# Stream 1 five weight chunks behind stream 0 at a layer's end and beginning, with seven weight buffers

## The chip, the cores and the metric

The kernel runs on one core of a Trainium2 chip. The metric is device time in microseconds (us) of one execution, less is better. Names of engines: TensorE is PE (its weight loads are PEld), VectorE is DVE, ScalarE is ACT, GpSimd is POOL, SyncE is SP.

## What is computed

Two requests of 128 tokens each run through the same two layers of width 2048: a context prompt (stream 0 here) and noisy latents (stream 1). A layer of the reference, cut to its matrix products:

```python
h = rms_norm(x, norm_w[l]) * (1 + scale) + shift          # scale, shift, gate: c @ w_mod[l]
parts = split_columns(h @ w_in[l])                        # 15872 columns
o_hg = hgrn_branch(...); o_at = attention(...); o_s5 = s5_branch(...)
merged = sum(sigmoid(merge) * (o @ w_br[l]))              # over the three branches
x = x + gate * (merged @ w_out[l])
```

After the last layer `rms_norm(x, final_norm)` is returned, with caches and states. `rms_norm` needs the sum of squares over all 2048 columns of a token, so neither the next layer nor the final scaling can start before the last output column of that token is there.

## The kernel before, in words

**Streams.** Tokens are rows: 128 partitions for stream `s = 0`, 128 for `s = 1`. Both use the same weights, so each weight chunk that is loaded serves both.

**A product in two parts.** Activations and weights in float32 are each split into a rounded part (`hi`, `wh`) and a remainder (`lo`, `wl`), and a product is the sum of three: `lo*wh`, `hi*wh`, `hi*wl` (lines 178 to 180). Weights move through the array (128x512), the activations are the stationary 128x128 operand.

**`gemm` (L160).** One group is 512 columns of the result for both streams, accumulated in two PSUM tiles `ps[0]`, `ps[1]` over `nk` chunks of 128 rows, 16 chunks for `w_in` and `w_out`. SP loads two chunks at a time (`raw`, 512 KB, three buffers, L168). ACT casts a chunk to `wh` (L138), DVE subtracts to get `wl` (L139), and PE does three products for stream 0 and then three for stream 1. `wh` and `wl` have four buffers each (`self.wp`, L68), so a chunk can be cast when the chunk four before it has been used by both streams.

**The end of a layer (L993 to L1025).** Four groups `n` of `w_out`. After each, and for each stream: DVE multiplies by the gate (`gb`, L1015) and adds the residual (L1016), ACT squares with a sum (`square`, L303). After `n = 3`, `token_rstd` (L305) reduces the eight partial sums of both streams in one 128x2 tile and computes 1/sqrt with one Newton step (`rstd`, L183: one ACT and six DVE instructions). In the last layer DVE also multiplies by `final_norm` (L1022) and `final` (L1060) scales the rows, stream 0 on DVE and stores on SP, stream 1 on ACT and stores on ACT's own queue.

**The beginning of a layer.** `normed` (L311) makes one quarter `q` of the normalised rows: DVE scales (`xn`, L322), PE transposes four blocks (L134), DVE (stream 0, L328) or ACT (stream 1, L330) applies scale and shift (`hf`), then cast and subtraction give `hh` and `hl`. Layer 1's first group is `("u", 0)`, 16 chunks, four for each quarter. In layer 0 the first groups are begun quarter by quarter (`begin`), since `w_mod` is still being loaded, so `group` finds `("u", 0)` already begun there.

**What sets the order.** The engines' queues are written by a planner that simulates the program: each instruction has a rank (`prio`, a smaller number goes first) and is placed when its operands are there in the plan. Weight loads and splits have `P_TOP` (1 million), the last column's chain and `token_rstd` `P_LAST` (0.9 million), `normed` `P_CHAIN` (2 million), S5 preparation 3 million, setup work `P_PREP` 5 million, weight products `P_PE` (6 million); within a rank program order decides. On the chip each engine runs its queue in order.

Of the kernel before, what the change touches and what calls it, by code (L numbers as in the profile page):

```python
# [15 lines left out]
ALU = mybir.AluOpType  # L16
AX = mybir.AxisListType
# [3 lines left out]
D = 2048  # L21
# [4 lines left out]
ROPE_THETA = 10000.0  # L26
NP = T // 2
RAW = 3
MB = 2
PTAGS = [(t, 2) for t in ("Bl", "S16", "ys")] + [(("k4", "k4"), 1)] + [("H8", 2)] * 4  # L30
STAGS = (("H8", 2),)
# [23 lines left out]
P_PE = 6_000_000  # L55
# [6 lines left out]
class Builder:  # L62
    def __init__(self, tc, ctx, io):
        self.tc, self.nc, self.io = tc, tc.nc, io
        self.seq = 0
        pool = lambda name, bufs, **kw: ctx.enter_context(tc.tile_pool(name=name, bufs=bufs, **kw))
        self.cp = pool("const", 1)
        self.wp = pool("weights", 4)  # L68
        self.sb = pool("sb", 1)
        self.bufs = dict(H8=4, Z8=2, Bl=1, CC=1, S16=1, uT=1, U2=1, ys=1, q4=2, kv=2,  # L70
                         mo=1, st=10, k2=6, k4=3, gt=4, sm=18, s5i=4, p=4, sb=1, sc=1, s5t=1)
        self.pg = pool("pg", 4, space=PSUM)
        self.pm = pool("pm", 2, space=PSUM)
        self.pb = pool("pb", 2, space=PSUM)
        self.dr = pool("scratch", 1, space=DRAM)
        self.uid = 0
# [80 lines left out]
        self.finish_side()  # L157
        self.side, self.side_rate, self.side_credit = gen, rate, 0.0

    def gemm(self, pieces, hi, lo, nk):  # L160

        nc = self.nc
        ps = [self.pg.tile([128, 512], F32, tag="g", name=self.nm("g")) for _ in range(2)]
        for kk, src in enumerate(pieces):
            self.side_work()
            with self.prio(P_TOP):
                raw = self.wp.tile([128, 2, 512], F32, tag="raw", name=self.nm("raw"), bufs=RAW)
                nc.sync.dma_start(raw, src.rearrange("p (a b) -> p a b", a=2))  # L168
            for j in range(2):
                with self.prio(P_TOP):  # L170
                    wh = self.wp.tile([128, 512], F32R, tag="wh", name=self.nm("wh"))
                    wl = self.wp.tile([128, 512], F32R, tag="wl", name=self.nm("wl"))
                    self.split_from(raw[:, j], wh, wl)
                k = 2 * kk + j
                with self.prio(P_PE):
                    for s in range(2):
                        sl = slice(s * 128, s * 128 + 128)
                        nc.tensor.matmul(ps[s], lo(k)[:, sl], wh, start=(k == 0), stop=False)  # L178
                        nc.tensor.matmul(ps[s], hi(k)[:, sl], wh, start=False, stop=False)  # L179
                        nc.tensor.matmul(ps[s], hi(k)[:, sl], wl, start=False, stop=(k == nk - 1))  # L180
        return ps

    def rstd(self, ssq, n, width):  # L183

        nc = self.nc
        v = self.ts("v", (128, n))
        y = self.ts("y", (128, n))
        r = self.ts("r", (128, n))
        w = self.ts("w", (128, n))
        nc.vector.tensor_scalar(v, ssq, 1.0 / width, EPS, ALU.mult, ALU.add)  # L190
        nc.scalar.activation(y, v, AF.Sqrt)
        nc.vector.reciprocal(r, y)
        nc.vector.tensor_mul(w, r, r)
        nc.vector.tensor_mul(w, w, v)
        nc.vector.tensor_scalar(w, w, -0.5, 1.5, ALU.mult, ALU.add)
        nc.vector.tensor_mul(r, r, w)
        return r
# [105 lines left out]
        self.nc.scalar.activation(junk, x[s][:, n * 512:(n + 1) * 512], AF.Square, accum_out=ssq[:, s, n:n + 1])  # L303

    def token_rstd(self, ssq):  # L305
        tot = self.ts("tot", (128, 2))
        self.nc.vector.tensor_reduce(tot, ssq, AX.X, ALU.add)
        r = self.rstd(tot, 2, D)
        return [r[:, s:s + 1] for s in range(2)]

    def normed(self, x, rs, q):  # L311

# [18 lines left out]
            sl = (slice(None), slice(q % 2 * 4, q % 2 * 4 + 4), slice(s * 128, s * 128 + 128))  # L331
            self.split_from(hf, self.hh[q // 2][sl], self.hl[q // 2][sl])

    def in_group(self, l, name, idx, k0=0, k1=16):

        pieces = [self.io["w_in"][l, GIDX[name, idx], kk] for kk in range(k0 // 2, k1 // 2)]
        return self.gemm(pieces, lambda k: self.hh[(k0 + k) // 8][:, (k0 + k) % 8],
                         lambda k: self.hl[(k0 + k) // 8][:, (k0 + k) % 8], k1 - k0)

    def add(self, dst, ps):  # L340
        with self.prio(P_TOP):
# [23 lines left out]
    def group(self, l, name, idx, func=None):  # L365
        dst = self.begun.pop((name, idx), None)
        if dst is None:
            ps = self.in_group(l, name, idx)
            dst = self.places(name, idx)
            for s in range(2):  # L370
                self.evac(ps[s], dst[s], func)
            return dst
        ps = self.in_group(l, name, idx, 8, 16)
        for s in range(2):
            self.add(dst[s], ps[s])
            if func is not None:
                with self.prio(P_TOP):
                    self.nc.scalar.activation(dst[s], dst[s], func)
        return dst
# [480 lines left out]
    def layer(self, l, x, rs):  # L860
        nc, io = self.nc, self.io
# [63 lines left out]
        for name, og in zip(("hg", "ag"), ogs):  # L925
            for hh in range(2):
                ps = self.in_group(l, name, hh)
# [7 lines left out]
        for b in range(3):  # L935
            if b == 1:
# [4 lines left out]
                def mods():  # L941
                    for p in parts:
                        yield from self.mod_part(*p, P_PE, tags, [("m", MB, MB)] * (8 // MB))

                if l + 1 < L:
                    self.start_side(mods(), MRATE[l] / MB)
                else:
                    self.start_side(self.gates, MRATE[l] / MB)
            if b == 2:
                sgs = {}  # L950
                for hh in range(2):
                    ps = self.in_group(l, "sg", hh)
# [4 lines left out]
            if b < 2:  # L957
                oh = self.t8("oh", (128, 8, 256), F32R)
                ol = self.t8("ol", (128, 8, 256), F32R)
                with self.prio(P_CHAIN):  # L960
                    for s in range(2):
                        for c in range(2):
                            tr = self.transpose4(ogs[b][s][c])
                            sl = (slice(None), slice(4 * c, 4 * c + 4), slice(s * 128, s * 128 + 128))
                            self.split_from(tr, oh[sl], ol[sl])
            else:
                early = [self.gate(l, b, n, ("st", "kv")[n]) for n in range(2)]
                oh, ol = self.s5_finish(l, ys, sgs)
                mt = [None] * 4
                m0 = self.t("S16", "mt", (128, 2, 8, 256), F32R)  # L970
                mt = [m0[:, 0], m0[:, 1]] + [self.t("H8", "mt", (128, 8, 256), F32R) for _ in range(2)]
            if merged is None:
                merged = [[self.t("st", "merged", (128, 512)) for _ in range(4)] for _ in range(2)]
            for n in range(4):
                gts = early[n] if b == 2 and n < 2 else self.gate(l, b, n, "gt")
                ps = self.gemm([io["w_br"][l, b, n, kk] for kk in range(4)],
                               lambda k: oh[:, k], lambda k: ol[:, k], 8)
                for s in range(2):
# [7 lines left out]
                    if b == 2:  # L986
                        with self.prio(P_CHAIN):
                            tr = self.transpose4(mb)
                            c = (4 * n) % 8
                            sl = (slice(None), slice(c, c + 4), slice(s * 128, s * 128 + 128))  # L990
# [3 lines left out]
        ssq = self.ts("ssq", (128, 2, 4))  # L994
# [4 lines left out]
                nc.gpsimd.dma_start(fn, bass.AP(src.tensor, src.offset, [[0, 128], [1, D]]))  # L999
        for n in range(4):  # L1000
            ps = self.gemm([io["w_out"][l, n, kk] for kk in range(8)],
                           lambda k: mt[2 * (k // 8)][:, k % 8], lambda k: mt[2 * (k // 8) + 1][:, k % 8], 16)
            sl = slice(n * 512, n * 512 + 512)
            if n == 3:
                self.finish_side()
                with self.prio(P_CHAIN):
                    nc.scalar.activation(self.ts("warm", (128, 1)), self.eye32[:, 0:1], AF.Sqrt)
            for s in range(2):
                with self.prio(P_LAST if n == 3 else P_TOP):
                    gb = self.t2("gb")  # L1010
                    nc.gpsimd.dma_start(gb, bass.AP(self.gate_d.tensor, self.gate_d.offset + (l * 2 + s) * D + n * 512,
                                                    [[0, 128], [1, 512]]))
                    xr = self.t2("xr")
                    nc.gpsimd.dma_start(xr, (io["x"] if l == 0 else self.x_d)[s][:, sl])
                    nc.vector.tensor_mul(gb, gb, ps[s])  # L1015
                    nc.vector.tensor_add(xn[s][:, sl], gb, xr)  # L1016
                    if l + 1 < L:
                        nc.gpsimd.dma_start(self.x_d[s][:, sl], xn[s][:, sl])
                    self.square(ssq, xn, s, n)
                if l + 1 == L:  # L1020
                    with self.prio(P_TOP + 500_000):
                        nc.vector.tensor_mul(xn[s][:, sl], xn[s][:, sl], fn[:, sl])  # L1022
        with self.prio(P_LAST):
            rs = self.token_rstd(ssq)
# [47 lines left out]
    def build(self):  # L1072
# [22 lines left out]
        for l in range(L):  # L1095
            x, rs = self.layer(l, x, rs)
            if l + 1 < L:
                def gates():
                    tags = itertools.cycle(MTAGS)
                    for p in (4, 5):  # L1100
                        yield from self.mod_part(L - 1, p, P_PE, tags, [("m", MB, MB)] * (8 // MB))

# [106 lines left out]
```

## Time and profile before

| | |
|---|---|
| median of 3 runs | 2330.3 us (2329.36 to 2330.72) |
| the profiled execution | 2331.88 us, its span 2330.1 us |
| granted TensorE clock, mean | 0.994 of full speed |
| PE busy | 2257.9 us, 97% |
| DVE busy | 1798.2 us, 77% |
| ACT busy | 1180.8 us, 51% |
| loaded from HBM | 474.36 MB, 207 GB/s over the span |

Times in the rows are us from the span's start. A busy share is an average; what an engine waited for, and in which stretch, is in the rows of the waits and of the timeline. `L178` is line 178 of the kernel; `wl<-raw,wh` is output from inputs; `x2` says how many instructions a row merges. In a timeline row the bracket at the end is the engine's idle time before it and what released it.

### The profile page before, as it was taken

The numbers are of one execution on the slowest core, as the hardware profiler recorded it, in microseconds if no ns is written. First come the engines' busy times: TensorE is split into PE (matmuls) and PEld (weight loads), VectorE is DVE, ScalarE is ACT, GpSimd is POOL, SyncE is SP. The second block draws the span as 40 slices with busy tenths as digits, with TensorE's granted clock in tenths as the row PEclk, the third lists the DMA queues.
The fourth block names the chain that finished last, engine by engine and source line by source line (L and its number), as shares of the span: only waits on it lengthen the run. The fifth ranks groups of instructions, "written<-read, shape, count | busy, mean of one in ns | idle before, by whom it ended". The sixth has DMA issues, their size and how long they took to land.

```text
span 2330.1 us, 38207 instructions
## 1 busy us (share of the span) xinstructions
PE 2257.9 (97%) x13192; PEld 1812.2 (78%) x13192; DVE 1798.2 (77%) x4835; ACT 1180.8 (51%) x2061; POOL 133.9 (6%) x244
## 2 busy tenths in 40 slices
PE   4999999999999999999998999999999999999997
PEld 2777877888887776887777888888878877887886
DVE  5856899799879868865565798899959968956555
ACT  3536645555554343544446565555564544454454
POOL 2000000100000100000010001000010010000000
PEclk9999999999999999999999999999999999999999
DMA  8994554355557878677874554454545677656765
GB/s 313 342 341 142 165 172 137 110 162 184 178 165 258 295 267 298 220 251 265 305 231 138 163 174 153 132 160 155 188 155 190 194 245 240 198 179 219 240 202 181
DMA packets 131490, 483.85 MB, mean 208 GB/s; under 512 B 17200, under 2 KB 17808, under 8 KB 126944
## 3 DMA queue, kind: packets, MB, share of 16 engines
q1 hardware_dynamic: 120528, 454.09, 58.2%
q0 software_dynamic: 9472, 23.97, 3.3%
q10 hardware_dynamic: 1296, 3.36, 0.4%
q8 instruction: 103, 1.69, 0.3%
q14 instruction: 91, 0.75, 0.1%
HBM read 474.36 MB, written 6.98 MB: 207 GB/s over the span
## 4 chain that ended last, share of the span: by engine, by line
PE 82%; DVE 8%; DMA 7%; issue 2%; ACT 1%; SPq 0%; POOL 0%; DVEq 0%; ACTq 0%; POOLq 0%
PE g L178 23%; PE g L180 23%; PE g L179 22%; DMA raw<-w_in 3%; DVE wl L139 3%; PE mod L274 3%; PE bu L816 3%; PE lv L432 2%; DMA raw<-w_br 2%; DMA wm<-w_mod 2%; PE tr L134 2%; PE yp L847 1%; DVE p L830 1%; DVE Sb L834 1%; ACT wh L138 1%
## 5 line engine op out<-in xcount | busy, mean ns | idle before, releaser
L138 ACT CAST wh<-raw 128x512 fp32r<-128x512 f32 x1344 | 819.4, 622 | 925.0 <-PE g L179 459.8
L139 DVE TENSOR_TENSOR wl<-raw,wh 128x512 fp32r<-128x512 f32 x1344 | 915.5, 689 | 368.5 <-ACT wh L138 319.1
L178 PE MATMUL g<-wh,hl 128*128 128x512 f32 x1984 | 785.1, 396 | 6.4 <-ACT wh L138 2.7
L179 PE MATMUL g<-wh,hh 128*128 128x512 f32 x1984 | 777.9, 392 | 0.0
L180 PE MATMUL g<-wl,hh 128*128 128x512 f32 x1984 | 700.9, 398 | 0.4 <-DVE wl L139 0.3
L178 PEld LDWEIGHTS g<-wh,hl 128*128 128x128 f32 x1984 | 373.5, 188 | 99.4 <-ACT wh L138 8.2
L179 PEld LDWEIGHTS g<-wh,hh 128*128 128x128 f32 x1984 | 373.6, 188 | 75.7 <-issue 0.2
L180 PEld LDWEIGHTS g<-wl,hh 128*128 128x128 f32 x1984 | 366.6, 189 | 82.5 <-DVE wl L139 5.8
L178 PE MATMUL g<-wh,ol 128*128 128x512 f32 x384 | 152.0, 396 | 2.5 <-ACT wh L138 2.3
L828 DVE TENSOR_TENSOR p<-s5sc,Sb 128x64 f32<-128x64 f32 x512 | 140.8, 275 | 14.9 <-ACT Sb L820 5.9
L179 PE MATMUL g<-wh,oh 128*128 128x512 f32 x384 | 149.9, 390 | 0.0
L834 DVE TENSOR_TENSOR Sb<-Sb,p 128x64 f32<-128x64 f32 x512 | 141.7, 277 | 8.9
L830 DVE TENSOR_TENSOR p<-s5sc,Sb 128x64 f32<-128x64 f32 x512 | 139.2, 272 | 0.0
L180 PE MATMUL g<-wl,oh 128*128 128x512 f32 x384 | 132.0, 393 | 0.8 <-DVE wl L139 0.8
L274 PE MATMUL mod<-wm,cs 128*32 128x256 f32 x1536 | 104.5, 404 | 26.6 <-DMA wm<-w_mod 20.1
L833 DVE TENSOR_TENSOR p<-p,p 128x64 f32<-128x64 f32 x512 | 113.6, 222 | 6.1
L274 PEld LDWEIGHTS mod<-wm,cs 128*32 128x32 f32 x1536 | 44.7, 113 | 77.1 <-DMA wm<-w_mod 24.1
L179 PE MATMUL g<-wh,mt 128*128 128x512 f32 x256 | 99.8, 390 | 0.0
L178 PE MATMUL g<-wh,mt 128*128 128x512 f32 x256 | 99.7, 389 | 0.0
L178 PEld LDWEIGHTS g<-wh,ol 128*128 128x128 f32 x384 | 72.1, 188 | 20.3 <-ACT wh L138 4.6
L180 PEld LDWEIGHTS g<-wl,oh 128*128 128x128 f32 x384 | 71.5, 188 | 17.6 <-DVE wl L139 2.4
L180 PE MATMUL g<-wl,mt 128*128 128x512 f32 x256 | 83.5, 393 | 1.7 <-DVE wl L139 1.7
(315 smaller groups left out, 2116.8 us busy)
## 6 DMA issues: line engine op xcount, KB each, us to landing
raw<-w_in SPq DMA_DIRECT2D x496, 512.0 KB, 3.8
wm<-w_mod SPq DMA_DIRECT2D x130, 512.0 KB, 7.2
raw<-w_br SPq DMA_DIRECT2D x96, 512.0 KB, 4.2
raw<-w_out SPq DMA_DIRECT2D x64, 512.0 KB, 4.3
wm<-w_mod SPq DMA_DIRECT2D x31, 1024.0 KB, 7.4
raw<-w_glu SPq DMA_DIRECT2D x16, 512.0 KB, 3.9
gb<-gate_d POOLq DMA_DIRECT2D x16, 256.0 KB, 6.0
x<-x ACTq DMA_DIRECT2D x2, 1024.0 KB, 14.0
```

The costliest lines, as they stand in the source:

```text
L134: nc.tensor.transpose(ps[:, k], src[:, k * 128:(k + 1) * 128], self.ident)
L138: self.nc.scalar.copy(hi, src)
L139: self.nc.vector.tensor_sub(lo, src, hi.bitcast(F32))
L178: nc.tensor.matmul(ps[s], lo(k)[:, sl], wh, start=(k == 0), stop=False)
L179: nc.tensor.matmul(ps[s], hi(k)[:, sl], wh, start=False, stop=False)
L180: nc.tensor.matmul(ps[s], hi(k)[:, sl], wl, start=False, stop=(k == nk - 1))
L274: nc.tensor.matmul(ps[32 * i:32 * i + 32, 0:256], self.cT[:, 2 * k:2 * k + 32], ws[k - 2 * k0][:, i * 256:i * 256 + 256], start=(k0 == kb ...
L816: nc.tensor.matmul(pps[x][:, j2, k], Bl[pr, d, ri, k, j2, :], U2[pr, j2, 2 * qh + k].rearrange("p s t -> p (s t)"), start=True, stop=True, ...
L828: tt(p0.rearrange("p d (j s) -> p d j s", s=2), view(sc, qd * 32, [[16, 2], [1, 16], [0, 2]]), view(Sb, i, [[ds, 2], [2 * W, 16], [W, 2]]) ...
L830: tt(p1, view(sc, 128 + qd * 64, [[32, 2], [16, 2], [1, 16]]), view(Sb, i + RI, [[ds, 2], [-RI, 2], [W, 16]]), ALU.mult)
L833: tt(p0, p0, p1, ALU.add)
L834: tt(cur, cur, p0, ALU.add)
```

## The change

- `gemm` takes a `lag`. Stream 0's three products of a chunk are issued at once, stream 1's are kept in a list and issued when more than `lag` chunks wait there; the rest follows after the last chunk. The products themselves are in a new function `products`.
- `lag` is 5 (`LAG`) in the last output group (`n == 3`) of both layers, and in group `("u", 0)` where `group` computes it whole, which is layer 1. It is 0 elsewhere.
- `wh` and `wl` have seven buffers instead of four, throughout the kernel.
- `token_rstd` reduces and computes 1/rms for each stream by itself.
- The scratch for dynamic DMA is set to 4096 bytes of a partition.

```diff
+LAG = 5
-        self.wp = pool("weights", 4)
+        self.wp = pool("weights", 7)
-    def gemm(self, pieces, hi, lo, nk):
+    def gemm(self, pieces, hi, lo, nk, lag=0):
         nc = self.nc
+        late = []
...
-                k = 2 * kk + j
+                late.append((2 * kk + j, wh, wl))
                 with self.prio(P_PE):
-                    for s in range(2):
-                        sl = slice(s * 128, s * 128 + 128)
-                        nc.tensor.matmul(ps[s], lo(k)[:, sl], wh, start=(k == 0), stop=False)
-                        nc.tensor.matmul(ps[s], hi(k)[:, sl], wh, start=False, stop=False)
-                        nc.tensor.matmul(ps[s], hi(k)[:, sl], wl, start=False, stop=(k == nk - 1))
+                    self.products(ps, hi, lo, nk, 0, *late[-1])
+                    if len(late) > lag:
+                        self.products(ps, hi, lo, nk, 1, *late.pop(0))
+        with self.prio(P_PE):
+            for chunk in late:
+                self.products(ps, hi, lo, nk, 1, *chunk)
         return ps
+
+    def products(self, ps, hi, lo, nk, s, k, wh, wl):
+        sl = slice(s * 128, s * 128 + 128)
+        mm = self.nc.tensor.matmul
+        mm(ps[s], lo(k)[:, sl], wh, start=(k == 0), stop=False)
+        mm(ps[s], hi(k)[:, sl], wh, start=False, stop=False)
+        mm(ps[s], hi(k)[:, sl], wl, start=False, stop=(k == nk - 1))
...
     def token_rstd(self, ssq):
-        tot = self.ts("tot", (128, 2))
-        self.nc.vector.tensor_reduce(tot, ssq, AX.X, ALU.add)
-        r = self.rstd(tot, 2, D)
-        return [r[:, s:s + 1] for s in range(2)]
+        rs = []
+        for s in range(2):
+            tot = self.ts("tot", (128, 1))
+            self.nc.vector.tensor_reduce(tot, ssq[:, s], AX.X, ALU.add)
+            rs.append(self.rstd(tot, 1, D))
+        return rs
...
-            ps = self.in_group(l, name, idx)
+            ps = self.in_group(l, name, idx, lag=LAG if (name, idx) == ("u", 0) else 0)
...
-                           lambda k: mt[2 * (k // 8)][:, k % 8], lambda k: mt[2 * (k // 8) + 1][:, k % 8], 16)
+                           lambda k: mt[2 * (k // 8)][:, k % 8], lambda k: mt[2 * (k // 8) + 1][:, k % 8], 16, LAG if n == 3 else 0)
...
-    nc = bacc.Bacc("TRN2", target_bir_lowering=False, num_devices=1)
+    nc = bacc.Bacc("TRN2", target_bir_lowering=False, num_devices=1, dynamic_dma_scratch_size=4096)
```

## Rows read from the trace of the kernel before

**Rows 1.** The page: PE's busy time, and the chain that ended last, by engine.

```profile
PE 2257.9 (97%) x13192; PEld 1812.2 (78%) x13192; DVE 1798.2 (77%) x4835; ACT 1180.8 (51%) x2061; POOL 133.9 (6%) x244
...
PE 82%; DVE 8%; DMA 7%; issue 2%; ACT 1%; SPq 0%; POOL 0%; DVEq 0%; ACTq 0%; POOLq 0%
```

**Rows 2.** Waits of PE over the span: total us, times, longest us.

```profile
PE mod L274 <- DMA wm<-w_mod: 20.1, 11, 4.7
PE tr L134 <- DVE xn L322: 10.4, 3, 6.5
...
PE g L178 <- ACT wh L138: 5.0, 8, 1.5
PE g L180 <- DVE wl L139: 2.7, 5, 1.0
...
PE g L178 <- DVE hl L139: 2.0, 6, 0.5
```

**Rows 3.** Stretches: length, busy PE, PEld, DVE, ACT, POOL, granted clock, DMA, GB/s.

```profile
1224.00:1227.00 3.00, 0.00 (x0) 0.00 (x0) 1.66 (x9) 1.00 (x5) 0.82 (x2) 0.75 0.88 249
...
1231.00:1233.00 2.00, 2.00 (x6) 1.60 (x6) 0.35 (x1) 1.67 (x5) 0.00 (x0) 0.50 0.00 0
...
45.00:50.00 5.00, 3.47 (x10) 2.61 (x11) 5.00 (x31) 2.75 (x6) 0.00 (x0) 0.50 1.03 423
```

**Rows 4.** Chain that ended last, in order of time: start us, us, what.

```profile
1232.66 0.43 PE g L178
...
2314.75 0.45 PE g L180 x2
```

**Rows 5.** Timeline of the boundary between the layers: start us, us, engine, line.

```profile
1220.01 0.62 PE L180 MATMUL g<-wl,mt 128*128 128x512 f32 x2
1220.94 1.28 DVE L1015 TENSOR_TENSOR gb<-gb,g 128x512 f32<-128x512 f32 x2
1222.14 0.69 DVE L139 TENSOR_TENSOR wl<-raw,wh 128x512 fp32r<-128x512 f32 x1
1222.74 1.29 DVE L1016 TENSOR_TENSOR x<-gb,xr 128x512 f32<-128x512 f32 x2
1223.46 0.63 ACT L303 ACTIVATE junk<-x 128x512 f32<-128x512 f32 x1 [2.64 <-DVE x L1016]
...
1226.45 0.49 DVE L322 TENSOR_SCALAR xn<-x,r 128x512 f32<-128x512 f32 x1
...
1227.09 1.08 PE L134 MATMUL tr<-ident,xn 128*128 128x128 f32 x4 [6.46 <-DVE xn L322]
1228.21 1.37 DVE L328 TENSOR_SCALAR hf<-tr,modT 128x128 f32<-128x128 f32 x4 [1.27 <-PE tr L134]
...
1230.26 0.69 DVE L139 TENSOR_TENSOR hl<-hf,hh 128x512 fp32r<-128x512 f32 x1 [0.29 <-ACT hh L138]
...
1231.01 0.80 PE L178 MATMUL g<-wh,hl 128*128 128x512 f32 x1
```

**Rows 6.** Timeline of the last output column of layer 0.

```profile
1198.60 0.62 ACT L138 CAST wh<-raw 128x512 fp32r<-128x512 f32 x1 [0.73 <-PE g L179]
...
1208.50 1.14 ACT L138 CAST wh<-raw 128x512 fp32r<-128x512 f32 x2 [3.83 <-DMA raw<-w_out]
...
1216.47 0.73 PE L180 MATMUL g<-wl,mt 128*128 128x512 f32 x2 [1.03 <-DVE wl L139]
```

**Rows 7.** Timeline of the tail; the last row is DMA issues, us to landing.

```profile
2316.38 1.29 DVE L1015 TENSOR_TENSOR gb<-gb,g 128x512 f32<-128x512 f32 x2 [4.32 <-PE g L180]
...
2321.77 1.33 ACT L1069 ACTIVATE x<-x,r 128x512 f32<-128x512 f32 x2 [1.02 <-DVE r L196]
...
2323.74 1.96 ACTq L1070 DMA_DIRECT2D o_y<-x  x2
...
o_y<-x ACTq DMA_DIRECT2D x4, 256.0 KB, 4.1
```

**Rows 8.** Timeline of the start: the first weight product of layer 0.

```profile
47.62 0.79 PE L178 MATMUL g<-wh,hl 128*128 128x512 f32 x1 [0.32 <-DVE hl L139]
```

More of the change, by code (lines that the diff above doesn't have):

```diff
@@ L332, in normed, with in_group @@
             self.split_from(hf, self.hh[q // 2][sl], self.hl[q // 2][sl])
-    def in_group(self, l, name, idx, k0=0, k1=16):
+    def in_group(self, l, name, idx, k0=0, k1=16, lag=0):
         pieces = [self.io["w_in"][l, GIDX[name, idx], kk] for kk in range(k0 // 2, k1 // 2)]
         return self.gemm(pieces, lambda k: self.hh[(k0 + k) // 8][:, (k0 + k) % 8],
-                         lambda k: self.hl[(k0 + k) // 8][:, (k0 + k) % 8], k1 - k0)
+                         lambda k: self.hl[(k0 + k) // 8][:, (k0 + k) % 8], k1 - k0, lag)
     def add(self, dst, ps):
```

## The prediction, made before the changed kernel ran

> **What bounds the kernel now.** The page first: TensorE (PE) is busy 2257.9 of 2330.1 us and holds 82% of the chain that ended last [rows 1]. A change can only take away time in which PE idles, or TensorE's low clock. Idle time is 2330.1 - 2257.9 = 72 us. The waits of PE [rows 2] say what ends it: 20.1 us for `w_mod` loads and 10.4 us, in three pieces, for the normalised rows `xn`; weights in splitting cost only 5.0 us (`wh`) and 2.7 us (`wl`), late `hl` 2.0 us. The largest single piece but for the start is the 6.46 us on `xn`, where layer 1 begins. [...] The chain of waits gives the pitch of a 128x512 product: 0.43 us there, 0.45/2 = 0.227 us elsewhere [rows 4]. The timeline [rows 5] has the boundary: the last products of layer 0's output columns end at 1220.6 (call it E), the first of layer 1 starts at 1231.01: 10.4 us. One chain fills them: gate, residual, squares, 1/rms, scaling, transposes, modulation, split. The tail has the same chain without successor: 2316.38 to 2330.1, 13.7 us [rows 7].
>
> **Part by part. The lag.** Each chunk of weights served stream 0 and at once stream 1. In the last of the four output columns of a layer (column 3) stream 1 now follows five chunks behind. After stream 0's last product come (5+1) x 3 = 18 products of stream 1, 18 x 0.227 = 4.1 us in which stream 0's chain runs beside PE; now it leads by one product (the two `hi*wl` stand last, side by side, [rows 5]), 0.23 us. No product is added.
>
> The written order is only a rank: the planner takes the highest-ranked product whose operands are there in its plan. That it departs from program order is seen in the same row: per stream the code has `lo*wh, hi*wh, hi*wl`, the trace has both `hi*wl` together, since `wl` comes after `wh`. With lag five a chunk is held for six chunks and seven buffers leave one ahead. The ring: a product frees the buffer for the cast (0.62 us, released by PE in [rows 6]), then the split `wl` takes 0.69 us [rows 5], 1.31 us and two hand-offs; the chunk is due 2 x 3 x 0.227 = 1.36 us after the release, its `wl` 2 x 0.227 = 0.45 us later still. So `wl` has under 0.5 us to spare. One other DVE instruction in between (a gate multiply takes 0.64 us) and stream 0's product isn't ready while stream 1's are: the plan takes those, and a chunk of lag is gone. Ends: lag 0 and 5. I take 3, nearer to the ring's having some room: 12 products, 2.7 us of lead.
>
> Stream 0's chain alone, from [rows 5]: gate and residual half of 1.28 and 1.29, together 1.29; squares to `xn` 2.99 less the second stream's square 0.63, 2.36; `xn` to transposes 0.64; these to modulation 1.12; on to `hl` 2.05; to the product 0.75. Sum 8.2 us. DVE takes stream 1's gate and residual (1.3 us, ranked above) in the middle, and a weight split as now (0.69 us, half counted). 8.2 + 1.3 + 0.35 = 9.85; the first product at E - 2.7 + 9.85 = E + 7.1, not E + 10.4: 3.3 us gained. With lag 5 stream 1's gate falls where stream 0 waits for transposes (0.5 us left): E - 4.1 + 9.05 = E + 5.0, 5.4 us. With no lag, 0.
>
> **The clock.** The dozen products after the gap now run at 0.43 us: 12 x 0.2 = 2.4 us lost. The idle stretch shrinks but does not go, so 0 to 2.4 us; I take 1.2. [...] If any idling brings the low clock the term is 0 and the time 1.2 us worse; if the shorter gap is forgiven it is 2.4 and the time 1.2 us better.
>
> **Lag in the first group of layer 1, seven buffers there.** Stream 0's and stream 1's four-chunk blocks already alternate, held by `hl`. Three more chunks can be split while PE idles. What is to be had is part of the 2.0 us for `hl` over the kernel; I take 0.5 (0 to 1).
>
> **1/rms per stream.** Seven DVE instructions and one of ACT more for each of three places. On stream 0's chain it takes off the second square, counted above. At the start it lies beside loads for which PE waits (20.1 us, [rows 2]): nothing. Without that cover it costs at most what the whole stretch from square to `xn` takes for one stream, 2.4 us.
>
> **The tail.** PE end to stream 1's scaling is now 2316.38 to 2321.77, 5.4 us, with both streams and the `final_norm` multiplies on DVE. Stream 1 alone: 1.29 + 2.36 = 3.65, plus one multiply 0.69 in the way: 4.3, 1.1 us less the 0.2 by which its last product ends later: 0.9. From the scaling to the end it is 8.3 us: eight stores of 256 KB compete, the last group of issues takes 1.96 us [rows 7]. Stream 0's four leave earlier; stream 1's needs 2.66 us for four scalings, an issue (0 to half of 1.96 us, 0.35 taken) and the landing, now 4.1 us beside all eight, taken at 3.7: 6.7, saving 1.6. Together 2.5; 3.1 with lag 5, 0.6 with none.
>
> **Seven buffers elsewhere, DMA scratch of 4 KB.** PE's waits for `wh` and `wl`, 7.7 us, are the most that deeper buffers can give; I take 1.0. They cost too: splits rank above the normalisation, and at the start DVE is full, 5.00 of 5.00 us in 45 to 50 [rows 3]; three more splits ahead of the first product are 3 x 0.69 = 2.1 us, less what would have been filler; I take 0.7 (0 to 2.1). In column 3 of layer 0 PE already idles for late `wl`, 1.03 us the longest, after a raw load kept ACT waiting 3.83 us [rows 6]; with one chunk ahead, not three, that could come to 3.4 us (five chunks used in 0.68 instead of 1.36 us each), or the 1.0 us go; I take 0.
>
> The smaller scratch I take at 0: the gate multiply at 1220.94 starts right after PE's last product, so gate loads come early enough now. The ends are 0 and 3.8 us, what a crowded load cost ACT in [rows 6].
>
> **Sum.** 3.3 + 1.2 + 0.5 + 2.5 + 1.0 - 0.7 = 7.8 us. The profiled execution took 2331.88 us (span 2330.1 and 1.8 around it): 2324.1. That execution is 1.6 us above the median 2330.3, so the forecast is 2330.3 - 7.8 = 2322.5 us.
>
> **Rivals.** *The lag survives whole.* For it: in pure weight stretches DVE has 0.69 us of splitting in each 1.36 us, so much of the time nothing stands in the way of `wl`. Against: one chunk of room. 5.4 + 2.4 + 0.5 + 3.1 + 0.3 = 11.7: 2318.6 us.
>
> *The lag isn't there.* The plan finds stream 1 ready and stream 0 not in each chunk, and the order stays as before. For it: the order seen now. Against: with seven buffers more is ready at once, so that rank decides. 0 + 0 + 0.5 + 0.6 + 0.3 = 1.4: 2328.9 us.
>
> *Splits ahead of the chain.* Seven buffers let three more splits run at the higher rank on DVE just where the normalisation needs it: 2.1 us at the start and 2.1 us at the boundary, and column 3 of layer 0 idles 3.4 us with its lookahead eaten, against 0.6 + 0.3 gained at the tail and elsewhere: +6.7 us, 2337.0 us. For it: DVE full in 45 to 50, the split within the chain at 1222.14 [rows 5]. Against: much DVE time there is filler that gives way. It decides if the first product of layer 0 starts over 1 us after 47.62 [rows 8] and that of layer 1 no earlier than E + 10.
>
> **How the numbers follow.** Forecast 0.45, whole lag 0.18, no lag 0.24, splits ahead 0.13. The measurement tells 0.2%, 4.7 us, from no change: faster is below 2325.6, slower above 2335.0. Of the forecast's case four fifths lie below 2325.6 (unknowns of some 3 us either way): 0.36 + 0.18 + 0.04 of the no-lag case (other waits gone) = 0.58. Slower: most of the last rival, 0.10, and 0.01 of the others: 0.11. The rest, 0.31, is no change. The range reaches from 2316 (whole lag and 2.6 us of the waits for weights) to 2332 (no lag, and 3 us of the costs).
>
> **What would show it.** Right: in column 3 the two streams' products no longer alternate by chunk, `gb` of stream 0 starts 2 to 4 us before PE's last product, two `tot` reductions of 128x1, idle before the first transposes of layer 1 under 4 us (now 6.46), the low clock shorter; the same lead before the end, and stores of stream 0 issued some 2 us before stream 1's scaling. Wrong: `gb` still at PE's end (no lag); new idle time on `wl` or `wh` in column 3; the first product of layer 0 later. A shift of many us in stretches that no edit touches would mean that the plan has moved elsewhere, which this working can't price.

## The result, and the profile after

The changed kernel took 2345.05 us (2343.06 to 2348.56, four runs), the kernel before 2330.51 on the same chip: ratio 1.0064, 95% interval 1.0047 to 1.0082. It is slower by 14.5 us; the forecast was 2322.5, the range 2316 to 2332. The profiled execution took 2343.06 us, its span 2341.3: 11.2 us more than the span before. (A ratio here need not be exactly the quotient of the two medians.)

The page of the changed kernel, against [rows 1]: span, and busy time by engine.

```profile
span 2341.3 us, 38233 instructions
...
PE 2263.9 (97%) x13192; PEld 1824.3 (78%) x13192; DVE 1801.5 (77%) x4856; ACT 1176.3 (50%) x2065; POOL 132.1 (6%) x244
```

PE has the same 13192 instructions, is busy 6.0 us longer and idles 77.4 instead of 72.2 us. Where: layer 0's last product ends at 1229.0 (before 1220.6), layer 1's first product starts 12.3 us after it (before 10.4), the rest of layer 1 takes 1.8 us more, and from the last product to the end it is 12.6 us (before 13.5). 8.4 + 1.9 + 1.8 - 0.9 = 11.2. So most of the loss lies ahead of the first place that the lag touches.

Windows up to that place, the kernel before and then the changed one (us, busy PE, PEld, DVE, ACT, POOL, granted clock, DMA, GB/s):

```profile
0.00:1220.63 1220.63, 1173.40 (x7116) 920.32 (x7116) 932.58 (x2621) 596.81 (x1045) 80.97 (x147) 1.00 0.67 228
182.00:188.00 6.00, 5.39 (x27) 4.33 (x28) 3.21 (x8) 3.28 (x8) 0.00 (x0) 1.00 0.06 21
387.00:393.00 6.00, 4.50 (x23) 3.75 (x22) 5.71 (x16) 3.17 (x5) 0.02 (x1) 1.00 0.28 87
592.00:598.00 6.00, 6.00 (x29) 4.97 (x28) 5.79 (x20) 2.52 (x5) 0.00 (x0) 1.00 0.76 262
```

```profile
0.00:1229.02 1229.02, 1175.84 (x7116) 929.41 (x7116) 936.13 (x2628) 597.15 (x1048) 81.78 (x147) 0.98 0.65 227
182.00:188.00 6.00, 4.05 (x14) 3.04 (x13) 3.60 (x11) 2.74 (x6) 0.68 (x1) 0.54 0.08 25
387.00:393.00 6.00, 4.58 (x22) 4.08 (x21) 4.51 (x19) 3.53 (x5) 0.00 (x0) 0.52 0.26 89
592.00:598.00 6.00, 4.34 (x14) 3.46 (x15) 4.04 (x12) 3.15 (x6) 0.75 (x1) 0.50 0.13 46
```

The same 7116 instructions: 6.0 us more idle (53.2 against 47.2) and 2.4 us more busy. The second number is a balance. Near 182, 387, 592 and 988 us the changed kernel has stretches at a granted clock of 0.50, where before has 1.00; one window for each of the four, summed:

```profile
sum 23.88, PE 18.67 PEld 15.11 DVE 15.52 ACT 9.79 POOL 3.37; mean PE 4.67 PEld 3.78 DVE 3.88 ACT 2.45 POOL 0.84
```

At 0.43 us for a product instead of 0.227 [rows 4] about half of these 18.67 us of PE is the price of the low clock, an estimate of 9 us. All the rest of PE's work up to the boundary then took some 7 us less than before; what saved that stays open.

PE's waits in the same two stretches, before and then changed (total us, times, longest):

```profile
PE g L178 <- ACT wh L138: 3.8, 6, 1.5
PE g L180 <- DVE wl L139: 2.5, 4, 1.0
PE tr L134 <- DVE bm L279: 2.3, 2, 1.7
```

```profile
PE tr L135 <- ACT sts L503: 5.2, 1, 5.2
PE tr L135 <- DVE bm L291: 5.1, 3, 2.0
PE yp L861 <- DVE Sb L848: 2.9, 1, 2.9
...
PE lv L434 <- DVE ks L429: 1.8, 1, 1.8
...
PE tr L135 <- DVE glu L1066: 1.3, 2, 0.7
```

The waits for weights, 6.3 us, are gone, as seven buffers should do. In their place stand 14 us (2.8 more on `bm`, 5.2 + 2.9 + 1.8 + 1.3 new) for branch work that PE had not caught up with before; the waits that both kernels have are 1.7 us shorter together. The longest, in the timeline of the changed kernel:

```profile
587.77 0.60 PE L135 MATMUL tr<-ident,q 128*128 128x128 f32 x4
...
589.62 1.28 ACT L203 ACT_TABLE_LOAD   x1
...
591.13 1.28 ACT L400 ACT_TABLE_LOAD   x1
...
592.92 0.58 ACT L503 COPY sts<-st 128x512 f32<-128x512 f32 x1
...
593.56 1.69 PE L135 MATMUL tr<-ident,q 128*128 128x128 f32 x5 [5.19 <-ACT sts L503]
```

PE's next weight products (`g<-wh,ol` at 595.54) need what comes of these transposes, and ACT works off sigmoid, square root, sigmoid, with a table load of 1.28 us at each change, before the copy that PE waits for.

The boundary, against [rows 5] (start, us, engine, line; idle time before and its releaser):

```profile
1228.41 0.61 PE L193 MATMUL g<-wl,mt 128*128 128x512 f32 x2
...
1230.61 0.69 DVE L140 TENSOR_TENSOR wl<-raw,wh 128x512 fp32r<-128x512 f32 x1 [0.67 <-ACT wh L139]
1231.22 0.68 DVE L1029 TENSOR_TENSOR gb<-gb,g 128x512 f32<-128x512 f32 x1
1231.81 0.68 DVE L140 TENSOR_TENSOR wl<-raw,wh 128x512 fp32r<-128x512 f32 x1
...
1237.39 1.08 PE L135 MATMUL tr<-ident,xn 128*128 128x128 f32 x4 [8.37 <-DVE w L205]
...
1240.42 1.08 PE L135 MATMUL tr<-ident,xn 128*128 128x128 f32 x4 [1.95 <-DVE xn L336]
...
1241.31 0.79 PE L191 MATMUL g<-wh,hl 128*128 128x512 f32 x1
```

There is no lead: both streams' last products stand side by side, as before. And the gate multiply starts 2.2 us after them, behind a split of layer 1's weights that waits for its cast; more splits stand inside the chain. The order of the 96 products in layer 0's last column (0 and 1 are the streams) shows what became of the lag:

```
000000000000000001101001111011111111111110011010011000100000000010000110011111111100011111111101
```

Stream 0 gets 17 products ahead while the prefetched chunks last; then stream 1's products come in front of its next one, which by the ranks means that this one wasn't ready in the plan, and they run until the lag is used up. It builds up and collapses twice, the second time at the end.

### The profile page after: what moved, and what is told of

The parts are those of the page before. It is cut to its first block, busy times and chain, and to the rows that moved or that the text cites. A ratio compares the mean times of both kernels' runs of the same rounds, so it can differ in the third digit from the quotient of the medians.

```text
span 2341.3 us, 38233 instructions
## 1 busy us (share of the span) xinstructions
PE 2263.9 (97%) x13192; PEld 1824.3 (78%) x13192; DVE 1801.5 (77%) x4856; ACT 1176.3 (50%) x2065; POOL 132.1 (6%) x244
## 4 chain that ended last, share of the span: by engine, by line
PE 90%; DVE 5%; DMA 3%; issue 1%; ACT 1%; SPq 0%; DVEq 0%; ACTq 0%
PE g L191 25%; PE g L192 25%; PE g L193 25%; PE mod L286 3%; PE bu L830 3%; PE lv L446 2%; PE tr L135 2%; DVE wl L140 2%; PE yp L861 2%; DMA raw<-w_in 2%; DMA wm<-w_mod 1%; PE bt L748 1%; PE yp L854 1%; DVE p L844 0%; DVE Sb L848 0%
## 5 line engine op out<-in xcount | busy, mean ns | idle before, releaser
L193 PE MATMUL g<-wl,hh 128*128 128x512 f32 x1984 | 778.7, 394 | 0.0
L193 PEld LDWEIGHTS g<-wl,hh 128*128 128x128 f32 x1984 | 373.5, 188 | 80.2 <-issue 2.3
L193 PE MATMUL g<-wl,oh 128*128 128x512 f32 x384 | 150.2, 393 | 0.0
L193 PE MATMUL g<-wl,mt 128*128 128x512 f32 x256 | 98.7, 390 | 0.0
## 6 DMA issues: line engine op xcount, KB each, us to landing
x<-x ACTq DMA_DIRECT2D x2, 1024.0 KB, 14.5
```

The lines of the kernel that those rows point to most:

```text
L193: mm(ps[s], hi(k)[:, sl], wl, start=False, stop=(k == nk - 1))
```

## The experiments

Diffs are against the kernel before unless said. "Boundary" is the time from layer 0's last product to layer 1's first, "tail" from the last product to the end, both from the profiled executions; "lead" is how long before PE's last product ends stream 0's gate multiply starts.

**The parts one by one (e1 to e4).**

```diff
e1 +nc = bacc.Bacc(..., dynamic_dma_scratch_size=4096)
e2  e1, and token_rstd per stream
e3  e1, and
   -self.wp = pool("weights", 4)
   +self.wp = pool("weights", 7)
e4  the changed kernel with
   -LAG = 5
   +LAG = 0
```

> The kernel before with the 4096-byte DMA scratch alone (four buffers, no lag, 1/rms of both streams together). [...] Theory A (the seven buffers cost the time): 2330.5 us, within 1 us of before, PE's waits as before. Rival B (the smaller scratch holds up POOL's loads of gates, biases and residuals): a good part of the 14.5 us, at least 5 us, and the new waits on bm (5.1 us in the changed kernel, 2.3 before) appear here.

> The scratch and 1/rms per stream, four buffers, no lag. PE, POOL and SP have the order of before; DVE and ACT differ only in the three places where 1/rms is computed. Theory A: within 1.5 us of before; at the start the first weight product about 1 us later than 47.62 (seven more DVE instructions in front of it), the tail up to 1.5 us shorter. Rival C (1/rms per stream costs the start and the boundary): 3 us or more above before, with the first product of layer 0 at 49.0 and the boundary over 11.5 us, as in the changed kernel (49.04 and 12.3).

> The scratch and seven buffers; no lag, 1/rms of both streams together. The orders differ from before on every engine, all over the kernel. Theory A (seven buffers let weight splits run further ahead, and the planner then places all other work otherwise): most of the 14.5 us is here, 2340 to 2346 us, with new low-clock stretches near 182, 387, 592 and 988 us and the wait of 5.2 us on sts near 593. Rivals B and C: below 2335 us.

> The changed kernel with LAG = 0 (seven buffers, scratch, 1/rms per stream). Its orders differ from the changed kernel's only in the last output column of each layer and at the start of layer 1. Theory A: 2343 to 2347 us, within 2 us of the changed kernel, since no lag is left at a column's end there either. Rival D (the disordered products of the lagging columns cost time): at least 3 us below the changed kernel's 2345, the difference within 1190 to 1245 and 2295 to 2341 us.

| | median us | before, same chip | ratio, 95% interval |
|---|---|---|---|
| e1 scratch | 2334.14 | 2332.24 | 1.0004 (0.9990 to 1.0018) |
| e2 and 1/rms per stream | 2334.61 | 2332.24 | 1.0007 (0.9995 to 1.0020) |
| e3 scratch, seven buffers | 2344.77 | 2332.24 | 1.0051 (1.0033 to 1.0069) |
| e4 all but the lag | 2345.84 | 2332.24 | 1.0052 (1.0035 to 1.0070) |

Theory A holds: seven buffers alone bring 12 us of the loss. Scratch and 1/rms per stream change nothing in the total that can be measured, so rivals B and C are out. Rival D is out too: e4, without the lag, takes as long as the changed kernel, so what was left of the lag has no cost that can be measured. The late start comes with the buffers: the first product is at 47.23 in e2, 48.11 in e3, and 1/rms per stream adds 0.9 us to seven buffers (49.03 in e4, 49.04 in the changed kernel). e3 has the idle places of the changed kernel (PE waits 5.2 us for `sts`, 4.4 for `Sb`, 5.1 for `bm`). In the built programs, e1 has the order of before on every engine and e2 on PE, SP and POOL. In e3, 8647 of PE's 10936 places hold another instruction than in e1, from the 104th on.

**Is it the depth, or the order that the planner draws? (e7, e8, e9, e14)** e7 and e8 are e3 with five and six buffers. In e9 and e14 the program is planned with four or six buffers, and its order is then imposed on the same program with seven:

```diff
+_, order = _program(bacc, arrays, 4, None)      # e14: 6
+nc, _ = _program(bacc, arrays, 7, order)
...
+for ks in order:                                # one list per engine
+    for a, b in zip(ks, ks[1:]):
+        tc.add_manual_dep(traced[b], traced[a].name, NoSync)
```

> The scratch and five buffers, no lag, 1/rms together. Theory H (each buffer more lets splits run further ahead at the cost of other work, in proportion): a third of the 12 us of seven buffers, 2335 to 2338 where before is at 2332, with part of the idle at 182, 386, 594 and 990 us. Rival I (any other plan is another draw, depth has no sign): anywhere within 10 us of before, with idle places that seven buffers do not have.

> As the run with five, with six buffers. Theory H: two thirds of the 12 us, 2338 to 2342. Rival I: not between five and seven, in time or in its idle places.

> Seven buffers and the scratch, as in e3, but every engine's instructions are held in the order that the planner gave the kernel with four buffers (edges between neighbours on each engine). No lag, 1/rms together. Theory J (the order is what costs the 12 us, the buffers themselves cost nothing): not above before, 2328 to 2333 us where before is at 2332; PE's waits for wh shorter than the 5.0 us of before, no waits near 594 or 988 us, low-clock stretches only where before has them. Rival K (seven buffers cost by themselves, through where they lie or what the transfers do): 2338 us or more, with waits at the places of e3.

> Seven buffers, every engine held in the order planned for six (e8). Theory J (the order alone makes the time): within 2 us of e8, 2324 to 2328 us where before is at 2333. Rival K (seven buffers cost some 4 us by themselves, as e9 left open): 2329 us or more.

| buffers, order | median us | before, same chip | ratio, 95% interval |
|---|---|---|---|
| e7 five | 2341.04 | 2333.03 | 1.0037 (1.0024 to 1.0051) |
| e8 six | 2325.47 | 2333.03 | 0.9971 (0.9961 to 0.9982) |
| e9 seven, order of four | 2336.57 | 2332.89 | 1.0017 (1.0003 to 1.0030) |
| e14 seven, order of six | 2323.73 | 2331.85 | 0.9970 (0.9957 to 0.9982) |

Depth has no sign: five lose, six gain, seven lose. Six and seven buffers in one order take the same time, which rival K can't explain. e9, with the order of before on PE, ACT, DVE and SP, loses a third of what e3 loses, though, against theory J's "not above before". Its interval overlaps with that of e1 (0.9990 to 1.0018), which has the same order and scratch with four buffers, so this remainder is not shown to be the buffers'. Its windows show where its profiled execution lost time:

```profile
592.00:598.00 6.00, 6.00 (x30) 4.94 (x29) 5.83 (x20) 2.76 (x6) 0.00 (x0) 1.00 0.51 175
934.00:940.00 6.00, 5.63 (x41) 3.76 (x42) 3.63 (x13) 3.52 (x6) 0.00 (x0) 0.72 0.87 283
1194.00:1200.00 6.00, 5.50 (x17) 4.38 (x18) 3.88 (x6) 3.25 (x6) 0.00 (x0) 0.72 0.72 227
```

The stall near 593 is gone with the order, but two stretches at a granted clock of 0.72 follow waits of 2.73 us (on a `w_mod` load) and 1.97 us (on weights). In the execution of before PE waits 0.3 us for `w_mod` between 925 and 945. Whether these two waits are due to the buffers stays open.

**The lag, held by an edge (e5, e6).** e5 regroups only the last four chunks of a column, on four buffers; e6 is the changed kernel with its lag of five enforced. Both compute 1/rms per stream.

```diff
+def behind(self, lag, ins, ps, hi, lo, nk, chunk):
...
+    with self.tc.issue_after(ins.ins):           # ins: stream 0's last product so far
+        self.products(ps, hi, lo, nk, 1, *chunk)
...
e5 -                    if len(late) > lag:
   +                    if len(late) > (0 if 2 * kk + j < nk - lag else lag):   # lag 4
```

> Four buffers as before, scratch and 1/rms per stream as changed. In each layer's last column only the last four chunks are regrouped: stream 0's twelve products, then stream 1's twelve, and this order on PE is forced by an edge (issue_after) instead of left to the rank. Theory E (the idea of the lag is sound, it failed since a rank could not hold it): stream 0's gate multiply about 2.7 us (12 x 0.227) before PE's last product; idle before layer 1's first transposes 3 to 4 us instead of 6.5; 4 to 8 us less than before in all. Rival F (the chain of stream 1, or stream 0's splitting work, ends last anyway): less than 2 us gained. Rival G (the forced order makes PE wait for wl within the column): idle on wl of 2 us or more in the last four chunks.

> The changed kernel with the lag of five held by an edge on PE: stream 1's products of chunk k-5 stand behind stream 0's last product of chunk k. Everything else as changed, seven buffers. Theory E: PE's order shows 18 products of stream 1 after stream 0's last; 4 to 8 us below the changed kernel, but still above before, as seven buffers cost what e3 showed (12 us). Rival G (one chunk ahead is too little for a forced order): idle on wl in the last columns of 3 us or more each, and no gain over the changed kernel.

e5: 2332.85 us (before 2333.03), ratio 0.9999 (0.9988 to 1.0010). e6: 2347.91, 1.0061 (1.0046 to 1.0077), no better than the changed kernel. The lead was there on PE (2.76 us in e5) and the total gained nothing. e5's timeline:

```profile
1217.85 2.57 DVE L750 TENSOR_TENSOR Sb<-Sb 64x256 f32<-64x256 f32 x6
...
1220.45 0.69 DVE L140 TENSOR_TENSOR wl<-raw,wh 128x512 fp32r<-128x512 f32 x1
...
1221.20 0.69 PE L200 MATMUL g<-wl,mt 128*128 128x512 f32 x1 [1.80 <-DVE wl L140]
...
1224.80 0.69 DVE L1036 TENSOR_TENSOR gb<-gb,g 128x512 f32<-128x512 f32 x1 [1.57 <-PE g L200]
...
1228.26 0.68 DVE L140 TENSOR_TENSOR wl<-raw,wh 128x512 fp32r<-128x512 f32 x1
...
1231.66 1.09 PE L135 MATMUL tr<-ident,xn 128*128 128x128 f32 x4 [4.10 <-DVE w L212]
```

Idle before the transposes fell from 6.46 to 4.10 us, the boundary from 10.4 to 8.0 and the tail from 13.5 to 11.6. Against e2, which lacks the block alone (9.8 and 13.0), the lead gives 1.8 and 1.4 us: theory E is right in kind, but below its 4 to 8 us. It was paid back ahead of the boundary: layer 0 ended 6.9 us later (1227.55 against 1220.63). 2.1 us of that is rival G: the forced products wait for splits that stand behind S5 work of layer 1 on DVE (1.29 and 1.80 us, before 1.03), and the seven products behind the second wait last 0.63 to 0.79 us each, those just ahead of it 0.39 or 0.40. The rest includes low-clock stretches where nothing was edited (0.72 in 182 to 188 and in 391 to 397, before 1.00; last section). In e6 the gate multiply stood behind eight such instructions and a split, and the boundary was 12.0 us.

**Splits out of the chain's way (e10, e13).** In e8, as in the changed kernel, the gate multiply stands on DVE behind a split, which waits for a cast, which waits for a load:

```profile
1211.05 0.61 PE L193 MATMUL g<-wl,mt 128*128 128x512 f32 x2
1213.61 1.14 ACT L139 CAST wh<-raw 128x512 fp32r<-128x512 f32 x2 [3.17 <-DMA raw<-w_in]
1214.26 0.69 DVE L140 TENSOR_TENSOR wl<-raw,wh 128x512 fp32r<-128x512 f32 x1 [0.80 <-ACT wh L139]
1214.87 1.28 DVE L1027 TENSOR_TENSOR gb<-gb,g 128x512 f32<-128x512 f32 x2
```

```diff
e10 (on e8), e13 (on the changed kernel): in layer 1's first group
-                    self.split_from(raw[:, j], wh, wl)
+                    with self.tc.issue_after(self.first_xn) if hold and 2 * kk + j >= 2 else nullcontext():
+                        self.split_from(raw[:, j], wh, wl)
```

> Six buffers (e8), and the weight splits of layer 1's first group from the third chunk on stand behind the first xn on DVE, by an edge. Four rows of DVE's order are moved and nothing else. Theory L (at the boundary the gate multiply of the last column stands on DVE behind splits that wait for casts and these for raw loads: in e8 it starts 3.2 us after PE's end): the gate multiply starts within 0.3 us of PE's last product, idle before the first transposes 6 to 6.7 us instead of 9.34, 2.5 to 3.5 us less than e8 (2325.5): 2322 to 2323. Rival M (the splits are only moved and PE then waits for wl in layer 1's first group): the first product earlier, but 2 us or more of new idle on wl, no gain.

> The changed kernel, and the splits of layer 1's first group from the third chunk on behind the first xn on DVE (as e10). Only a few rows of DVE's order move. Theory L: the gate multiply, 2.2 us late in the changed kernel, comes at PE's end; idle before the transposes 5.5 to 6.5 us instead of 8.37; 2 to 3 us below the changed kernel (2345): 2342 to 2343, so the boundary is the smaller part of the 14.5 us. Rival M: no gain, idle on wl later.

e10: 2322.65 us, 0.9952 (0.9937 to 0.9968), 2.8 us below e8's median; but its boundary is only 1.0 us shorter (12.3 against 13.3), and the intervals overlap, so the rest isn't shown to be the edit's. e13: 2348.08, 1.0075 (1.0061 to 1.0090), a miss: the gate multiply came on time, but the casts, which the edge on DVE does not hold, stood on ACT in front of the squares (`tot` waits 2.86 us for them), and the held splits then stood between `xn` and `hf`, so the boundary was 13.4 us. Moved work has to go somewhere that isn't the chain.

**The order of the boundary written out (e11, e12, e15, e16),** all with six buffers, the block of four and 1/rms per stream.

```diff
e11 = e10 + e5's block
e12 = e11, s5_input of layer 1 behind the third quarter's hl
e15 = e11 without its hold, and edges (later, first):
+ DVE: (gb of stream 1, first xn), (v of stream 1, first hl),
+      (splits of chunks 2, 3, first hl), (splits from chunk 4, xn of stream 1)
+ ACT: (casts from chunk 2, y of stream 0)
+ PE:  (transposes of stream 1, products of chunk 1), (products of chunk 2, those transposes)
+ stream 1's last square writes a scratch tile of its own
e16 = e15, s5_input of layer 1 behind the last hl
```

> e10 with the forced block of the last four chunks (as e5) and 1/rms per stream. Theory E': with splits out of the way the lead of stream 0 (2.7 us) reaches the first product: idle before the transposes 3 to 4 us, 2 to 5 us less than e10. Rival N (S5 work of layer 1 stands on DVE among the last column's splits, so stream 0's twelve products wait for wl as in e5): idle on wl of 2 us or more in the last column, and no gain over e10.

> e11, and the first S5 input block of layer 1 stands on DVE behind the third quarter's hl, out of the last column. Theory E'': no idle on wl in the last column; 3 us or more below e11 if rival N holds there. Rival I again (the plan of layer 1 moves, as one more draw): a difference of either sign, up to 10 us, with idle places in layer 1 (after 1260 us) that e11 does not have.

> e11 with the boundary's order written out by edges: on DVE stream 1's gate multiply behind stream 0's first xn, stream 1's 1/rms and the splits from the third chunk on behind stream 0's first hl, those from the fifth behind stream 1's first xn; on ACT the casts from the third chunk on behind stream 0's square root; on PE stream 1's first transposes between the second and third chunk of stream 0's first products. Theory O (in e11 the lead of 2.8 us was spent on stream 1's steps and splits that stood in front of stream 0's chain, and on stream 1's transposes in front of stream 0's first product): from stream 0's gate multiply to its first product 8.5 to 9.5 us instead of 12.05, the first product 2.5 to 3.5 us earlier, 2 to 3 us below e11 (2322.5). Rival P (stream 1's chain, pushed back, then holds PE in its turn): the first product as early, but idle before stream 1's transposes or its first products of the same size, no gain.

> e15 with the first S5 input block of layer 1 behind the last hl of the normalisation, out of the last column. If the idle of 2.26 us on wl in e11's last column and the low clock that follows cost what they seem to: 2 to 4 us below e15. Rival I (the plan of layer 1 is drawn anew behind it): either sign, with idle places after 1260 us.

| | median us | ratio, 95% interval | lead | boundary | tail |
|---|---|---|---|---|---|
| e10 | 2322.65 | 0.9952 (0.9937 to 0.9968) | -1.1 | 12.3 | 13.1 |
| e11 | 2322.47 | 0.9955 (0.9941 to 0.9969) | 2.8 | 9.3 | 11.6 |
| e12 | 2326.01 | 0.9972 (0.9960 to 0.9985) | 2.7 | 8.2 | 11.6 |
| e15 | 2320.08 | 0.9950 (0.9937 to 0.9964) | 1.3 | 7.0 | 11.7 |
| e16 | 2321.07 | 0.9956 (0.9944 to 0.9968) | 2.7 | 5.6 | 11.6 |

The kernel before took 2332.89 us beside e10 to e12 and 2331.85 beside e15 and e16. In e11 a lead of 2.8 us becomes a first product 9.3 us after PE's end. Its timeline shows the lead being spent:

```profile
1219.29 0.69 DVE L1039 TENSOR_TENSOR gb<-gb,g 128x512 f32<-128x512 f32 x1 [1.41 <-PE g L201]
...
1219.90 0.15 DVE L329 TENSOR_REDUCE tot<-ssq 128x1 f32<-128x4 f32 x1
...
1223.63 1.89 DVE L140 TENSOR_TENSOR wl<-raw,wh 128x512 fp32r<-128x512 f32 x3
1225.43 0.41 DVE L352 TENSOR_SCALAR hf<-tr,modT 128x128 f32<-128x128 f32 x1
...
1227.15 0.49 DVE L344 TENSOR_SCALAR xn<-x,r 128x512 f32<-128x512 f32 x1
...
1227.79 1.09 PE L135 MATMUL tr<-ident,xn 128*128 128x128 f32 x4 [3.97 <-DVE xn L344]
```

Stream 1's gate multiply, which has to wait for PE's last product, stands in front of stream 0's `tot`; with it and stream 1's residual, `xn` comes 2.4 us later after stream 0's gate multiply than in the prediction's sum (6.07 us, not 1.29 + 2.36). Behind `xn` another 1.4 us go: splits stand in front of `hf`, stream 1's `xn` in front of `hl`, and on PE stream 1's transposes in front of stream 0's first product (0.3 us at most: `hl` ends at 1228.25, the product starts at 1228.53). e15 puts these behind:

```profile
1213.81 0.67 DVE L1058 TENSOR_TENSOR gb<-gb,g 128x512 f32<-128x512 f32 x1
...
1218.21 1.09 PE L135 MATMUL tr<-ident,xn 128*128 128x128 f32 x4 [3.12 <-DVE xn L356]
...
1221.39 0.69 DVE L141 TENSOR_TENSOR hl<-hf,hh 128x512 fp32r<-128x512 f32 x1 [0.62 <-ACT hh L141]
...
1222.13 0.80 PE L210 MATMUL g<-wh,hl 128*128 128x512 f32 x1 [2.84 <-DVE v L221]
...
1224.86 1.08 PE L135 MATMUL tr<-ident,xn 128*128 128x128 f32 x4
```

From gate multiply to first product it is 8.3 us, in e11 12.05: theory O's place and size, and stream 1's transposes at 1224.86 wait for nothing, so rival P isn't there. Its lead is only 1.3 us, since two splits stand in front of the gate multiply. e15 is the fastest by its median, 11.8 us below before; its interval does not separate it from e10, e11 and e16. e16 has the boundary down to 5.6 us and gives it back by e15's measure: the rest of layer 1 is 4.9 us longer in its profile. PE idles 1.1 us more in it (a wait for `hl` of 1.15 us at 1225.37) and is busy 3.8 us longer with the same products, which stays open. e12 likewise gained at the boundary and lost in layer 1 (a wait of 3.80 us for `wl` at 1249.88).

## Why the prediction was wrong

**The step that failed: "Seven buffers elsewhere", taken at 1.0 us of gain.** That term looked at what deeper buffers can give, the waits for weights, and these did go. It took the rest of the plan as fixed. Seven buffers change which instruction is ready first in the planner, and so the order of the whole kernel; that draw cost 12 us (e3), another one gained some 7 (e8). Of the 22.3 us between the sum (7.8 gained) and the result (14.5 lost), 13.5 are this term. The prediction's last sentence named a moved plan as what its working can't price, and the range was drawn as if that were unlikely.

**"The written order is only a rank", then three chunks of lag taken to survive.** The premise was right and its consequence was the rival "the lag isn't there": measured, none survives at a column's end (the gate multiply starts 2.2 us after PE's end in layer 0, and 0.64 us before it in layer 1, as in e4 without lag). Forced, it lasts (e5, e6).

**Lag in the first group of layer 1, 0.5 us.** In the built program this group has the order of e4, without lag, and the waits for `hl` in it are 0.9 us (before 1.0): nothing.

**Stream 0's chain: 8.2 us alone, 9.85 with others' work.** Alone it is right: 8.3 us in e15 and e16. With others the planner's order puts in 2.6 us (e5: 10.8) to 4.9 us (e6: 13.1), not 1.65. The pieces priced too low are DVE's: in e5 four splits, not half of one, stand with stream 1's gate and residual between stream 0's residual and its `xn`, and that is the whole 2.6 us; in e11 stream 1's gate multiply holds up the chain until PE ends. PE's own queue, which the sum left out, costs at most 0.3 us (e11). What the second square takes off (0.63) is there without any lag: the boundary is 9.8 us in e2 and 10.4 in e1.

**The clock, 1.2 us taken as regained.** The amount was the author's choice between 0 and 2.4 us, and no run shows it. The low clock stayed: where before has 0.75 and 0.50 at the boundary [rows 3], the changed kernel has 0.50 (1234 to 1237 and 1241 to 1243), and so has e15 (1222 to 1224), with idle pieces of only 3.12 and 2.84 us. What fell in the changed kernel is the number of slow products: six (0.58 to 0.79 us each, from 1241.31), in before eleven (0.53 to 0.80 us, from 1231.01), an estimate of 5 x 0.2 = 1.0 us, but behind a boundary that is 1.9 us longer. What was missing is the opposite sign: in the changed kernel new low-clock stretches came with new idle places (0.50 in 592 to 598, the end of 5.19 us of idling and the products behind it, where before has 1.00). Four such stretches cost 9 us by the estimate above, and the sum had no term for it.

**The tail, 2.5 us.** The changed kernel gained 0.9 of it, without a lead; 1/rms per stream alone 0.5 (e2: 13.0); with a lead of 2.7 us it is 1.9 to 2.0 (e5, e11). Right in kind, a little large. In the changed kernel stream 0's scalings and stream 1's small steps share DVE, so stream 1's scaling comes 7.3 us after the gate multiply, not 5.4 [rows 7], and the gain is behind it (6.0 us to the end, not 8.3):

```profile
2328.01 1.37 DVE L1029 TENSOR_TENSOR gb<-gb,g 128x512 f32<-128x512 f32 x2 [4.68 <-PE g L193]
...
2333.58 1.84 SPq L1081 DMA_DIRECT2D o_y<-x  x4
...
2335.30 1.33 ACT L1083 ACTIVATE x<-x,r 128x512 f32<-128x512 f32 x2 [2.35 <-DVE r L208]
```

**The start, 0.7 us of cost,** was 1.4 (49.04 against [rows 8]), inside its bounds. **The scratch, 0,** was right (e1).

**The rivals.** "Splits ahead of the chain" had the sign and met its condition (first product 1.4 us late, layer 1's at E + 12.3), at the boundary with 1.9 us for its 2.1. Its third piece, 3.4 us in column 3, did not appear, and of the 8.4 us ahead of the boundary all but the 1.4 of the start were in no rival. That its sign came out is largely luck: its 2337.0 is 8 us short, and most of the loss lies elsewhere.

## What to carry to other kernels

Where a planner writes the order, a change of buffer depth is a new draw for the whole kernel, here from -7 to +12 us: compare the orders of the two programs before pricing anything, and hold the old order if only the depth is to be judged. An order that must hold, such as a lag, needs an edge; a rank gives way whenever the other work is ready first. And a lead of one stream pays only if every queue on its chain (here DVE above all, ACT in e13, PE least) serves it first: 2.8 us of lead brought the first product at E + 9.3 or, in order, at E + 7.0 with half that lead (e15) and at E + 5.6 with all of it (e16).

## What was unexpected in the hardware

In these runs the low clock does not follow from the idle pattern alone. e1 and e2 have the same order on PE, and PE idles alike: 0.71 us and then 1.95 us, which end at 181.24 in e1 and 181.73 in e2. The windows behind, e1 and then e2:

```profile
181.00:187.00 6.00, 5.50 (x27) 4.48 (x28) 3.23 (x9) 3.30 (x8) 0.00 (x0) 1.00 0.09 26
181.00:187.00 6.00, 5.27 (x21) 4.33 (x22) 2.37 (x5) 2.74 (x6) 0.00 (x0) 0.72 0.14 49
```

e5 and before differ in the same way near 390 us: both wait 1.42 and then 1.50 us, and the granted clock in 391 to 397 is 0.72 and 1.00. A program with before's order on every engine (e1) ran between 2327.1 and 2338.8 us, and the clock is a part of such a spread: of 79 executions of the kernel before, the six with a mean granted clock of 0.996 took 2326.6 to 2327.9 us and the six with 0.990 took 2331.8 to 2337.2. It isn't all of it: 16 with 0.993 took 2328.3 to 2341.9.

The prediction has no term for a change of the activation table. In the trace of the changed kernel one cost 1.3 us: the load at 589.62 takes 1.28 us, and the square root follows at 590.91. All 47 loads of this trace take 1.28 us, and all but the first, at 2.15, start within 0.03 us of the end of the instruction before, so 1.3 us is the price here.
